# Gates o and z as token-major strips of seven products; branch gates and convolutions as filler in the attention, their results in DRAM

## The chip, the core and the metric

One core of a Trainium2 chip runs the whole program. The engines are TensorE (PE, matmuls and transposes, with its weight loads as PEld), VectorE (DVE), ScalarE (ACT), GpSimd (POOL) and SyncE (SP, which here only issues DMA transfers). The metric is the device time of one execution in microseconds, less is better. Times are the median of several runs; the profile and the trace come from one profiled execution.

## The reference

A decoder block on 512 tokens of 1024 channels, in fp32. Its columns of `w_in` make an mLSTM branch (4 heads of 256), a sparse-attention branch (8 heads of 64) and two merge gates.

```python
hN = _rmsnorm(x, norm_g)
p = _split_in(hN @ w_in)          # m_q m_k m_v m_o m_z: 1024 columns each; g_a g_b: 1024 each; the rest for attention
mq = silu(_causal_dwconv(p["m_q"], conv_q_w, conv_q_b))     # 4 taps along the tokens
mk = silu(_causal_dwconv(p["m_k"], conv_k_w, conv_k_b))
mh = _head_layernorm(_mlstm(mq, mk, p["m_v"], i, f), mh_norm_g)
ya = sigmoid(p["m_o"]) * mh * silu(p["m_z"])
yn = _nsa(...)                                               # compressed, selected and sliding attention, gated
yb = yn * silu(p["n_z"])
merged = sigmoid(p["g_a"]) * (ya @ w_branch_a) + sigmoid(p["g_b"]) * (yb @ w_branch_b)
return _rmsnorm(x + merged @ w_out, final_norm_g)
```

## The kernel before

**Products.** Every fp32 operand is split into a high part (`wh`, `hTh`) and a low part (`wl`, `hTl`), and a product is three matmuls: high by high, high by low, low by high (L214, L216, L218). The normalised input stands in SBUF as `hTh` and `hTl`, [128, 8, 512]: channel within a block, block, token. `weights` (L156) loads 512 KB of raw weights by SyncE's queue into `wr`; ScalarE copies the high part to `wh`, VectorE subtracts for the low part `wl` (L145). Each of the three has three buffers.

**Jobs and filler.** `cols(c0, post)` (L222) makes a job: 128 columns of `w_in` with all tokens, 8 blocks by 3 = 24 matmuls of 512 columns into one PSUM bank, and then `post`, which works on the bank. The result is channel-major, [128 channels, 512 tokens]. Jobs go into `stream` (class `Stream`, L176), which runs the load and the split of a job's weights ahead of its matmuls and gives out the matmuls one step at a time. Attention and mLSTM take such steps between their own matmuls, so that PE has work while the other engines prepare the next of its operands: `tick` (L984) takes 4 steps, or work of the side list; mLSTM takes 6 after a piece of a head (`stream.step(6)`) and 30 before the transposes of a head (`NORM_FILL`). PE, GpSimd and SyncE get their final order from a scheduler; ScalarE and VectorE keep the order of the program (`ordered`, L84).

**The stages** and when they run, by the trace: the start with normalisation and transposes (0 to 30 us); the first projections (30 to 77); attention (77 to 271), 16 units in the loop at L1031, with filler from the stream; two branch-gate jobs (271 to 284); the value strips (284 to 322); four convolution jobs (322 to 343); four mLSTM heads (343 to 499, each some 41.6 us, loop at L1314); branch a with the last gates (499 to 560); the output product (560 to 613) and the tail.

**What fills attention.** `some` (L759) adds eight o jobs and eight z jobs. `gate_o` (L591) puts tanh of its half into `gate` [128, 8, 512]; `gate_z` (L594) multiplies the z path's SiLU, made from a tanh, onto it. Two more jobs there are branch gates: `gate_ab` (L572) keeps sigmoid's tanh for g_a or g_b in SBUF until `branch_a` or `branch_b` uses it. `chores` (L1012) forms sums of quarters of the value columns in DRAM: `begin_sum` copies a quarter by SyncE's queue, `add_to_sum` adds another onto it by an accumulating DMA of GpSimd.

**Strips.** The values (512 x 1024 by 1024 x 1024) are token-major and split 2 by 2 by 2 in each of two token halves' sums: seven products of quarters, with sums of the input (`sum_of_h`, L1132) and of the weights, take the place of eight. `strip_product` (L1190) is one of the seven: two pieces of weights (`wr` of 512 KB each, two blocks by 512 columns), 12 matmuls for each of two row blocks of tokens; 24 in all. The banks are named X, Y and V, and each product's `post` stores a result or copies a partial sum.

**Convolutions.** `conv` (L1251) is a job whose `post` makes four taps along the tokens: one ScalarE pass, three VectorE passes on shifted columns, tanh, one VectorE pass for the SiLU, and the split into high and low. Four of the 16 run ahead of the heads, twelve as filler inside the head before the one that uses them; at a head's end the stream is run until the next head's four are done.

**The rest.** `branch_b` (8 jobs of 12 matmuls) fills the last head. `branch_a` (L1450) multiplies `ya` by `w_branch_a` and merges; six of the g_a gates are computed between its jobs. The output product is again one of seven products; its three weight sums T1, T2, T3 are formed on VectorE while branch a runs (`combine`, L1415; `w21`, L1574), and x for the residual is loaded meanwhile (`fetch_x`, L1485).

Of the kernel before, what the change touches and what calls it, by code (L numbers as in the profile page):

```python
# [28 lines left out]
EARLY = 2  # L29
FIRST = 2  # L30
AHEAD = 6
# [47 lines left out]
def build(  # L79
# [212 lines left out]
    with tc.tile_pool(name="ph0", bufs=2, side="right") as p0, tc.tile_pool(  # L292
# [230 lines left out]
        dve.tensor_scalar(prm[:, :, 10], prm[:, :, 10], 0.25, None, OP.mult)  # L523
# [48 lines left out]
    def gate_ab(base, j, pl):  # L572
        def post(ps):
            s = pl.tile([128, T], F32, name="s", tag="s", bufs=AHEAD if pl is not ybp and pl is not sg0 else 2)
            A(s, ps, AF.Tanh, scale=0.5)
            halves[base, j] = s

        cols(base + j * 128, post)

    gtp = tc.tile_pool(name="gtp", bufs=1, side="right")  # L580
    gate = gtp.__enter__().tile([128, ND, T], F32, name="gate")
# [8 lines left out]

    def gate_o(ct):  # L591
        cols(MO + ct * 128, lambda ps: A(gate[:, ct], ps, AF.Tanh, scale=0.5))

    def gate_z(ct):  # L594
        def post(ps):
            z = rpp.tile([128, T], F32, name="z", tag="z", bufs=1)
            silu2(z, ps, rpp, "slt", 1)
            dve.scalar_tensor_tensor(gate[:, ct], gate[:, ct], 1.0, z, OP.add, OP.mult)

        cols(MZ + ct * 128, post)  # L600
# [156 lines left out]
    gl_ = [(fn, ct) for ct in range(ND) for fn in (gate_o, gate_z)]  # L757

    def some(n):  # L759
        for _ in range(n):  # L760
            if gl_:
                fn, ct = gl_.pop(0)
                fn(ct)

    for base in (GA, GB)[:EARLY]:
        gate_ab(base, 0, ybp)
        if base == GA:
            first_layer(1, 1)
    some(2)
    queries(1)  # L770
    some(3)
    queries(2)
    some(4)
    queries(3)
    some(7)
# [84 lines left out]
    cmp_pool.__exit__(None, None, None)  # L860

# [128 lines left out]
    def new_p():  # L990
# [5 lines left out]
    dram = ctx.enter_context(tc.tile_pool(name="dram", bufs=1, space=bass.MemoryType.DRAM))  # L996
    wsum = [dram.tile([128, 4, 512], F32, name=f"wsum{n}") for n in range(4)]
    wq = [
        [wv[:, 4 * i : 4 * i + 4, MV + 512 * j : MV + 512 * j + 512] for j in range(2)] for i in range(2)
    ]  # L1000

    def begin_sum(n, src):
        tc.keep_in_program_order(nc.sync.dma_start(wsum[n], src))

    def add_to_sum(n, src):
        for q in range(2):
            part = slice(2 * q, 2 * q + 2)
            tc.keep_in_program_order(
                nc.gpsimd.dma_start(wsum[n][:, part], src[:, part], accum_op=OP.add)
            )  # L1010

    chores = deque(  # L1012
        (
            lambda: begin_sum(0, wq[0][0]),
            lambda: begin_sum(2, wq[0][1]),
            lambda: add_to_sum(0, wq[0][1]),
            lambda: begin_sum(1, wq[1][1]),
            lambda: add_to_sum(2, wq[1][1]),
            lambda: begin_sum(3, wq[1][0]),
            lambda: add_to_sum(1, wsum[0]),  # L1020
            lambda: None,
            lambda: add_to_sum(3, wsum[1]),
        )
    )
# [7 lines left out]
    for i, (c, hh, b) in enumerate(units):  # L1032
# [10 lines left out]
        if chores and i > 1:  # L1043
            chores.popleft()()
# [28 lines left out]
    stream.drain()  # L1073
    ap_.__exit__(None, None, None)
# [24 lines left out]
    sg0 = ctx.enter_context(tc.tile_pool(name="sg0", bufs=1))  # L1099
    in_turn = [j for i in range(4) for j in (i, i + 4)]  # L1100
    later = [(GB, 1), (GA, 4)] + [(GB, j) for j in range(2, ND)] + [(GA, j) for j in in_turn[2:]]
    ahead = deque(later[: FIRST + AHEAD])

    def gates_ahead(n, pl):
# [209 lines left out]
    for h in range(4):  # L1314
# [75 lines left out]
        if h < 3:  # L1390
            stream.run()
# [345 lines left out]
```

## Time and profile before

| | us |
|---|---|
| median of 3 runs (lowest, highest) | 623.44 (623.15, 624.19) |
| the profiled execution | 622.71 |
| its span, first to last instruction | 620.8 |
| bytes read from DRAM / written | 68.64 MB / 10.49 MB |
| PE in the start, 0 to 30 us | 27.74 busy |
| PE in the first projections, 30 to 77 us | 47.00 busy of 47.00 |

"Busy" is the time in which at least one instruction of an engine is under way. In a row of a group there stand line, engine, operation, output and inputs, shape, count, then busy us, mean ns of one instruction, and the idle time ahead of them with what ended it. Line 94 is the helper through which ScalarE, VectorE and GpSimd are called, so that groups are told apart by names and shapes. Matmuls overlap in PE: the duration of one is longer than the distance between two.

### The profile page before, as it was taken

Reading aid. Unit: us, or ns where it says so; the run is one execution under the profiler, and the core shown is the slowest. Engines: PE = TensorE matmul, PEld = TensorE weight load, DVE = VectorE, ACT = ScalarE, POOL = GpSimd, SP = SyncE. Lnnn points to the kernel's source line nnn. Section 1 sums busy time; section 2 is a strip of 40 time slices with the busy share of each in tenths; the row PEclk is TensorE's granted clock in tenths of the full one; section 3 lists DMA queues with packets and bytes.
Section 4 is the critical chain, followed back from the end, with each engine's and each line's share of the span. In section 5 each row is a group of like instructions: output and inputs, shape, how many; then the busy total and the mean of one; then the engine's idle time right before and its main releaser. Section 6 shows DMA issues by size and latency. Waiting matters only on the chain.

```text
span 620.8 us, 8484 instructions
## 1 busy us (share of the span) xinstructions
PE 609.2 (98%) x3033; PEld 507.3 (82%) x3033; DVE 449.1 (72%) x860; ACT 326.7 (53%) x621; POOL 85.3 (14%) x167
## 2 busy tenths in 40 slices
PE   8999999999999999999999999999999999999995
PEld 6988888888788888778888888888888888888884
DVE  5876766875876766669677888687787655458885
ACT  5675555556656656646654735545455232234654
POOL 6320012232341231220000000000000100000013
PEclk9999999999999999999999999999999999999999
DMA  9546535338625622123663223223132275333413
GB/s 297 166 112 184 126 104 196 86 91 198 136 57 114 134 71 68 35 68 125 200 185 103 68 69 101 69 69 101 35 101 70 79 247 167 101 106 122 129 34 137
DMA packets 92986, 72.34 MB, mean 117 GB/s; under 512 B 3168, under 2 KB 80132, under 8 KB 92944
## 3 DMA queue, kind: packets, MB, share of 16 engines
q1 hardware_dynamic: 90702, 66.55, 36.8%
q0 software_dynamic: 1664, 4.19, 4.3%
q10 hardware_dynamic: 578, 1.05, 0.5%
q8 instruction: 24, 0.39, 0.3%
q14 instruction: 18, 0.15, 0.1%
HBM read 68.64 MB, written 10.49 MB: 127 GB/s over the span
## 4 chain that ended last, share of the span: by engine, by line
PE 53%; DVE 2%; POOL 1%; ACT 1%; issue 0%; ACTq 0%; DVEq 0%; POOLq 0%
PE pp L218 12%; PE pp L214 12%; PE pp L216 12%; PE ps L174 1%; DVE s L94 1%; PE pp L1206 1%; PE pp L1208 1%; PE pp L1210 1%; PE ps L173 1%; PE ps L172 1%; PE pt L1354 1%; PE pt L1356 1%; PE pt L1355 1%; PE pt L1380 1%; PE pt L1210 1%; PE pt L1208 1%
## 5 line engine op out<-in xcount | busy, mean ns | idle before, releaser
L214 PE MATMUL pp<-hTh,wh 128*128 128x512 f32 (+1 forms) x488 | 191.5, 392 | 0.0
L216 PE MATMUL pp<-hTl,wh 128*128 128x512 f32 (+1 forms) x488 | 190.9, 391 | 0.0
L218 PE MATMUL pp<-hTh,wl 128*128 128x512 f32 (+1 forms) x488 | 190.6, 391 | 0.0
L94 DVE TENSOR_TENSOR wl<-wr,wh 128x1024 fp32r<-128x1024 f32 x92 | 113.2, 1232 | 40.9 <-ACT wh L94 39.5
L94 ACT ACTIVATE wh<-wr 128x1024 fp32r<-128x1024 f32 x92 | 97.2, 1057 | 77.1 <-PE pp L216 48.4
L218 PEld LDWEIGHTS pp<-hTh,wl 128*128 128x128 f32 x488 | 91.9, 188 | 16.5
L214 PEld LDWEIGHTS pp<-hTh,wh 128*128 128x128 f32 x488 | 91.9, 188 | 16.0
L216 PEld LDWEIGHTS pp<-hTl,wh 128*128 128x128 f32 x488 | 92.0, 189 | 15.7
L94 POOL TENSOR_SCALAR P<-P,st,gates 128x128 f32<-128x128 f32 (+1 forms) x64 | 45.3, 721 | 178.7 <-DVE st L94 132.2
L94 ACT ACTIVATE P<-P,st 128x128 f32<-128x128 f32 (+3 forms) x64 | 35.8, 559 | 37.9 <-DVE st L94 37.4
L94 DVE CUSTOM_DVE_ANT_0 P<-ps,cst 128x128 f32<-128x128 f32 (+3 forms) x64 | 30.4, 486 | 22.9 <-PE ps L939 21.8
L94 ACT ACTIVATE pth<-pt 128x512 fp32r<-128x512 f32 (+1 forms) x64 | 26.8, 434 | 28.9 <-PE pt L955 22.2
L94 DVE TENSOR_TENSOR ptl<-pt,pth 128x512 fp32r<-128x512 f32 (+1 forms) x64 | 30.1, 483 | 14.4 <-ACT pth L94 14.3
L94 DVE SCALAR_TENSOR_TENSOR u<-pp,prm,u 128x511 f32<-128x511 f32 (+2 forms) x48 | 35.7, 745 | 0.8
L94 POOL TENSOR_TENSOR rlr<-va,mhalf 128x4 f32<-128x4 f32 x4 | 5.1, 1285 | 208.6 <-DVE va L94 208.6
L94 ACT ACTIVATE th<-u 128x512 f32<-128x512 f32 x16 | 10.1, 631 | 39.5 <-DVE u L94 39.5
L955 PE MATMUL pt<-cst,P 128*128 128x128 f32 x160 | 28.9, 277 | 1.6 <-POOL P L94 1.0
L955 PEld LDWEIGHTS pt<-cst,P 128*128 128x128 f32 x160 | 20.1, 141 | 11.6 <-DVE ptl L94 4.9
L214 PE MATMUL pp<-yah,wh 128*128 128x512 f32 x64 | 24.9, 389 | 0.0
L216 PE MATMUL pp<-yal,wh 128*128 128x512 f32 x64 | 24.9, 389 | 0.0
L218 PE MATMUL pp<-yah,wl 128*128 128x512 f32 x64 | 24.9, 389 | 0.0
L968 PE MATMUL po<-ptl,vsw 128*128 128x512 f32 (+1 forms) x64 | 21.2, 332 | 0.0
(377 smaller groups left out, 1104.9 us busy)
## 6 DMA issues: line engine op xcount, KB each, us to landing
wr<-w_in SPq DMA_DIRECT2D x66, 512.0 KB, 3.9
wsum<-w_in SPq DMA_DIRECT2D x4, 1024.0 KB, 6.0
wr<-wsum SPq DMA_DIRECT2D x8, 512.0 KB, 4.3
wr<-w_out SPq DMA_DIRECT2D x8, 512.0 KB, 3.8
wr<-w_branch_a SPq DMA_DIRECT2D x8, 512.0 KB, 3.8
wsum<-w_in POOLq DMA_DIRECT2D x4, 512.0 KB, 8.2
wsum<-wsum POOLq DMA_DIRECT2D x4, 512.0 KB, 9.1
wr<-w_branch_b SPq DMA_DIRECT2D x4, 512.0 KB, 3.5
```

Source lines behind the costliest of these rows:

```text
L94: ins = fn(*args, **kw)
L172: pe.matmul(ps, a, c, start=start and i == 0, stop=False)
L173: pe.matmul(ps, a, d, start=False, stop=False)
L174: pe.matmul(ps, b, c, start=False, stop=stop and i == n - 1)
L214: pe.matmul(ps, a, c, start=k == 0, stop=False)
L216: pe.matmul(ps, a, d, start=False, stop=False)
L218: pe.matmul(ps, b, c, start=False, stop=k == nk - 1)
L955: pe.transpose(pt[:, (qb - kb) * 128 : (qb - kb) * 128 + 128], P[:, POFF[qb] + kb * 128 : POFF[qb] + kb * 128 + 128], ident,)
L968: pe.matmul(po[:, kb * 128 :], vl, tl[:, :n], start=False, stop=False)
L1206: pe.matmul(ps, a, c, start=begin, stop=False, skip_group_check=not first)
L1208: pe.matmul(ps, a, d, start=False, stop=False, skip_group_check=not first)
L1210: pe.matmul(ps, b, c, start=False, stop=k == 3, skip_group_check=not first)
```

## The change

**The o and z columns become strips.** `gate` is now [128, 4, 1024], token-major. The seven products of a strip are held in a class, once for each of v, o, z; `opening` makes the first two products, `rest` the other five.

```diff
-    for base in (GA, GB)[:EARLY]: ...
-    some(2) ... some(3) ... some(4) ... some(7)
+    class Strip:
...
+        def opening(self, pre=((), (), (), ())):
+            w = self.w
+            strip_product(of_h(0), from_w(w, 0, 0), self.X, True, self.after1, pre[:2])
+            strip_product(of_h(1), from_w(w, 1, 0), self.X, False, self.after2, pre[2:])
...
+            strip_product(of_sum(1), l5, self.V, True, self.after5, pre)
+            strip_product(of_sum(2), l6 if self.first is None else seeded, self.Y, False, self.after6)
+            strip_product(of_sum(3), l3, self.V, False, self.after3)
+            strip_product(of_sum(4), l7, self.Y, False, self.after7, whole=True)
+            strip_product(of_h(3), l4, self.Y, False, self.after4)
...
+    def put_o(tb, half, ps, part=None):
+        if part is not None:
+            dve.tensor_tensor(part, ps, part, OP.add)
+        g = gate[:, tb, half * 512 : half * 512 + 512]
+        A(g, ps if part is None else part, AF.Tanh, scale=0.5 if part is None else -0.5)
+
+    def put_z(tb, half, ps, part=None):
+        g = gate[:, tb, half * 512 : half * 512 + 512]
+        if part is None:
+            s = raws((0, 3)[tb % 2], (T,), "zs")
+            A(s, ps, AF.Silu)
+        else:
+            s = part
+            dve.tensor_tensor(s, ps, s, OP.add)
+            A(s, s, AF.Silu, scale=-1.0)
+        dve.scalar_tensor_tensor(g, g, 1.0, s, OP.add, OP.mult)
...
+    sv.opening(pre=((1,), (), (), ()))
+    so.opening(pre=((), (), (), (2,)))
+    sv.rest(pre=((3,), (4,)))
+    so.rest((o_sum1, lambda q: o_onto(1, 1, q), o_last, lambda q: halves_of(F[q]), lambda q: o_onto(1, 0, q)))
+    sz.opening()
+    sz.rest()
```

The sums of weights for v and z are made in DRAM during attention (16 chores, from unit 0 on, where nine stood from unit 2 on). Those for o are made in SBUF between the products, in a buffer E of 128 x 4 x 512 and two F:

```diff
+    def o_onto(i, j, q):
+        dve.tensor_tensor(piece_of(E, q), piece_of(E, q), raw_of(i, j, q), OP.add)
+        return halves_of(piece_of(E, q))
```

In the o strips' last five products PE's order, with the names' numbers kept (S20 and S21 are high and low part of a sum of the input, `wh` and `wl` a piece of the weights), reads:

```order
L1240 MATMUL pp_3545<-wh_3550,S20_3132 128x512
L1242 MATMUL pp_3545<-wl_3551,S20_3132 128x512
L1244 MATMUL pp_3545<-wh_3550,S21_3133 128x512
L1240 MATMUL pp_3543<-wh_3571,S20_3132 128x512
L1240 MATMUL pp_3545<-wh_3571,S20_3132 128x512
L1240 MATMUL pt_3554<-wh_3592,S30_3134 128x512
L1240 MATMUL pt_3561<-wh_3592,S30_3134 128x512
L1242 MATMUL pp_3543<-wl_3572,S20_3132 128x512
L1244 MATMUL pp_3543<-wh_3571,S21_3133 128x512
```

Four matmuls on two pieces' high parts (wh_3571, wh_3592) stand there ahead of the first on the low part wl_3572. Before, these columns were jobs inside attention.

**What fills attention now** is ten branch gates and eight convolutions, those of heads 0 and 1. Their results go to DRAM by SyncE's queue.

```diff
+    def gate_ab(base, j):
         def post(ps):
+            s = stg.tile([128, T], F32, name="s", tag="s", bufs=2)
             A(s, ps, AF.Tanh, scale=0.5)
+            away[base, j] = dram.tile([128, T], F32, name=f"away{base}_{j}")
+            nc.sync.dma_start(away[base, j], s)
...
+            both = pl.tile([128, 2, T], F32R, name="hl", tag="hl", bufs=2)
+            split(u, both[:, 0], both[:, 1])
+            if e == 0:
+                qk[i, h] = dram.tile([128, 2, 2, T], F32, name=f"qk{i}{h}")
+            nc.sync.dma_start(qk[i, h][:, :, e], f(both))
```

VectorE in attention, before, around a z job (z and gate are the job's; P, st the softmax, ptl the low half of the transposed probabilities, wl the low part of weights):

```order
L94 ISA P,st<-ps,cst 128x512
L94 ISA st 128x1
L94 RECIPROCAL st<-st 128x4
L94 TENSOR_TENSOR ptl<-pt,pth 128x512
L94 TENSOR_TENSOR wl<-wr,wh 128x1024
L94 SCALAR_TENSOR_TENSOR z<-sl,pp 128x512
L94 TENSOR_TENSOR ptl<-pt,pth 128x384
L94 SCALAR_TENSOR_TENSOR gate<-gate,z 128x512
```

And with the change, around a convolution (u, th and hl are its own; the three lengths 511, 510, 509 are the shifted taps):

```order
L92 TENSOR_TENSOR wl<-wr,wh 128x1024
L92 SCALAR_TENSOR_TENSOR u<-pp,prm,u 128x511
L92 TENSOR_TENSOR ptl<-pt,pth 128x128
L92 SCALAR_TENSOR_TENSOR u<-pp,prm,u 128x510
L92 ISA P,st<-ps,cst 128x128
L92 ISA st 128x1
L92 SCALAR_TENSOR_TENSOR u<-pp,prm,u 128x509
L92 ISA P,st<-ps,cst 128x128
L92 ISA st 128x1
L92 ISA P,st<-ps,cst 128x256
L92 ISA st 128x1
L92 SCALAR_TENSOR_TENSOR u<-th,u 128x512
```

Where two operations of a z job stood among the softmax's and the halves' operations, five of a convolution stand (the fifth, `hl<-u,hl`, follows some rows on).

**mLSTM.** The two gate jobs between attention and the strips are gone. After the strips come the four convolutions of head 2; those of head 3, the last six gates, all `branch_b` and the first six blocks of two `branch_a` jobs are the heads' filler (372 steps; the heads take 360), and the extra run at a head's end is gone. Each head reads its q and k back (`fetch_qk`), and two chores of the sums of `w_out` follow it:

```diff
+        if h < 3:
+            fetch_qk(h + 1)
+        for _ in range(2):
+            chores.popleft()()
...
+            nt = num[:, tb, 0:256]
+            A(nt, nt, AF.Identity, bias=nb[:, tb : tb + 1], scale=rho[:, tb : tb + 1])
+            dve.tensor_tensor(nt, nt, gate[:, tb, h * 256 : h * 256 + 256], OP.mult)
+        if h < 3:
+            decay(h + 1)
         stream.step(NORM_FILL)
...
+            gain = prm[:, ct, 10:11]
+            A(ya(ct), pt, AF.Copy, scale=gain)
+            dve.scalar_tensor_tensor(yal[:, ct], pt, gain, f(ya(ct)), OP.mult, OP.subtract)
-        while h < 3 and h + 1 not in done:
-            stream.step(1)
-        if h < 3:
-            stream.run()
```

SyncE's queue before, from the first convolution to branch a, held only weights:

```order
L159 DMA wr<-w_in 128x8x128 x22
L159 DMA wr<-w_branch_b 128x4x256 x4
```

With the change, where head 0's scores are done (qk00 to qk11 are the tiles of q and k, `wsumout` the sums of `w_out`, `away` a gate's place in DRAM):

```order
L1365 DMA qk00_4321<-qk01_2147 128x1024
L1365 DMA qk01_4322<-qk01_2147 128x1024
L1365 DMA qk10_4325<-qk11_2715 128x1024
L1365 DMA qk11_4326<-qk11_2715 128x1024
L1029 DMA wsumout1_4329<-w_out 512x1x512
L609 DMA qk03_4319<-hl_4316 256x1x512
L1029 DMA wsumout3_4331<-w_out 512x1x512
L580 DMA away6944_1_4415<-s_4413 128x512
L157 DMA wr_4569<-w_in 128x8x128
L157 DMA wr_4665<-w_in 128x8x128
```

Four reloads, two copies and two stores now stand ahead of the weights wr_4569.

**Branch a and the output product.** The six gate jobs there are gone; `branch_a` reads g_a's tanh and branch b's result from DRAM, and two of its jobs have only the last two blocks left. T1 to T3 are gone: the output product loads its weight sums from DRAM (`from_sums`), whose signs differ, so that `partway` and `piece` multiply one half by -0.5 and `sums` subtracts in another order. `AHEAD` goes from 6 to 8. In the whole program PE has 2975 matmuls in place of 3023.

More of the change, by code (lines that the diff above doesn't have):

```diff
@@ L756, in build @@
     first_layer(1, 0)
[L757 to L769, printed above, removed]
-    queries(1)
[L771 to L775, printed above, removed]
+    gate_job()
+    first_layer(1, 1)
+    gate_job(3)
+    queries(1)
+    for n in (1, 2, 3):
+        conv_job()
+        gate_job()
+        if n == 1:
+            conv_job()
+            queries(2)
+        elif n == 3:
+            conv_job()
+            queries(3)
+    for _ in range(3):
+        gate_job()
+        conv_job()
     def log_forget():
@@ L994, in new_p, with quarters, begin_sum, add_to_sum @@
         )
[L996 to L1005, printed above, removed]
+    def quarters(w, c0):
+        return [[w[:, 4 * i : 4 * i + 4, c0 + 512 * j : c0 + 512 * j + 512] for j in range(2)] for i in range(2)]
+    wov = w_out[0].rearrange("(k p) c -> p k c", p=128)
+    parts_of = {"v": quarters(wv, MV), "o": quarters(wv, MO), "z": quarters(wv, MZ), "out": quarters(wov, 0)}
+    wsum = {}
+    def begin_sum(w, n, src):
+        wsum[w, n] = dram.tile([128, 4, 512], F32, name=f"wsum{w}{n}")
+        tc.keep_in_program_order(nc.sync.dma_start(wsum[w, n], src))
+    def add_to_sum(w, n, src):
         for q in range(2):
@@ L1097, in build @@
         pool.memset(f(vals(h)[:, :, 257:258]), 0.0)
[L1099 to L1104, printed above, removed]
[L1105 to L1106 removed]
+    gtp = tc.tile_pool(name="gtp", bufs=1, side="right")
+    gate = gtp.__enter__().tile([128, NT, D], F32, name="gate")
     def quarter(t, i):
@@ L1463, in gen @@
                 me[j] = t
-                for i in range(4):
-                    if not left and i in me and i + 4 in me:
-                        sums(i)
-            stream.add(lambda: weights(wav[:, :, j * 128 : j * 128 + 128]), gen)
-        turns = deque(in_turn)
-        left = deque(later[FIRST + AHEAD :])
-        n = 0
-        while turns:
-            if left_to_add := later[FIRST + AHEAD + n : FIRST + AHEAD + n + 1]:
-                gate_into(*left_to_add[0], fp.tile([128, T], F32, name="g", tag="g", bufs=6))
-                if n in (1, 3):
-                    combine(n // 2)
-                n += 1
-                if n < 3:
-                    continue
-            branch_a(turns.popleft())
+                if j > 3:
+                    sums(j - 4)
+            stream.add(load, gen)
+        for j in in_turn:
+            branch_a(j)
         xo, fg = {}, {}
```

402 lines of the change are left out of this document (216 added, 186 removed).

## The prediction

> **What bounds the kernel now.** I read the page's head first, to see which engine has no spare time, and whether its clock is whole.
>
> ```profile
> span 620.8 us, 8484 instructions
> PE 609.2 (98%) x3033; PEld 507.3 (82%) x3033; DVE 449.1 (72%) x860; ACT 326.7 (53%) x621; POOL 85.3 (14%) x167
> PEclk9999999999999999999999999999999999999999
> ```
>
> TensorE is busy for 98% of the span at the full granted clock; VectorE, the next, has a quarter of its time free. The list of PE's waits says how much of the rest is waiting:
>
> ```profile
> PE ps L317 <- DMA grow<-norm_g: 2.3, 1, 2.3
> PE pt L955 <- POOL P L94: 1.0, 2, 0.6
> PE pt L955 <- DVE ptl L94: 0.5, 2, 0.3
> PE po L967 <- ACT pth L94: 0.3, 1, 0.3
> PE ps L691 <- PE pp L216: 0.3, 1, 0.3
> ```
>
> 2.3 us at the start, 2.1 us after it. So time leaves this kernel only with matmuls, and returns only with new waits of PE. The view by stretches of time shows where room is; its columns are each engine's busy us (instructions), the granted clock, the DMA share and GB/s. The stretches are attention, the two gate jobs behind it, the value strips, four convolution jobs, the four mLSTM heads, branch a, the output product, and the tail.
>
> ```profile
> 77.00:271.00 194.00, 191.73 (x1004) 157.50 (x1003) 136.43 (x331) 111.94 (x265) 53.12 (x72) 1.00 0.42 106
> 271.00:284.00 13.00, 13.00 (x60) 10.75 (x59) 10.18 (x11) 5.97 (x8) 0.33 (x8) 1.00 0.26 78
> 284.00:322.00 38.00, 38.00 (x169) 31.32 (x168) 30.63 (x32) 24.60 (x32) 0.00 (x0) 1.00 0.58 174
> 322.00:343.00 21.00, 21.00 (x95) 17.38 (x94) 15.58 (x21) 9.41 (x13) 0.00 (x0) 1.00 0.41 114
> 343.00:499.00 156.00, 156.00 (x783) 131.25 (x782) 121.41 (x237) 77.21 (x140) 5.14 (x4) 1.00 0.28 78
> 499.00:560.00 61.00, 61.00 (x270) 50.49 (x269) 32.88 (x42) 19.45 (x26) 0.00 (x0) 1.00 0.54 159
> 560.00:613.00 53.00, 53.00 (x244) 44.09 (x243) 44.52 (x62) 26.86 (x42) 6.12 (x17) 1.00 0.26 81
> 613.00:620.80 7.80, 0.71 (x6) 0.51 (x5) 3.24 (x11) 3.01 (x6) 2.09 (x6) 0.82 0.64 238
> ```
>
> PE idles 2.27 us in attention, and nowhere else between the start and the tail.
>
> **What PE loses.** The o and z columns were two products of 512x1024 by 1024x1024, 16 jobs of 24 matmuls of 512 columns. As strips of seven products each takes 7 x 24 = 168 matmuls where 192 stood. The order of instructions counts 3023 matmuls before and 2975 after; the 48 that go all have 512 columns, and every other shape keeps its count. A matmul's row says 0.39 us, but they overlap; what counts is the distance of the starts, here in the value strips:
>
> ```profile
> 299.80 0.39 PE L1206 MATMUL pp<-wh,S 128*128 128x512 f32 x1
> 300.03 0.39 PE L1208 MATMUL pp<-wl,S 128*128 128x512 f32 x1
> 300.26 0.39 PE L1210 MATMUL pp<-wh,S 128*128 128x512 f32 x1
> ```
>
> 0.23 us; over the stretch 284 to 322, 38.39 us (with the last one's 0.39) by 169 give 0.227. **48 x 0.227 = 10.9 us less.** That is sure as long as PE stays full, so the rest of the sum asks what it will wait for.
>
> **Attention (bound 0 to 17.9, taken 1.6).** Sixteen o and z jobs leave it, and eight convolutions and eight more branch gates enter it. Per job the other engines pay:
>
> ```profile
> L94 DVE SCALAR_TENSOR_TENSOR u<-pp,prm,u 128x511 f32<-128x511 f32 (+2 forms) x48 | 35.7, 745 | 0.8
> L94 DVE SCALAR_TENSOR_TENSOR u<-th,u 128x512 f32<-128x512 f32 x16 | 11.0, 686 | 7.1 <-ACT th L94 7.1
> L94 DVE TENSOR_TENSOR qkl<-u,qkh 128x512 fp32r<-128x512 f32 x16 | 11.0, 686 | 2.1 <-ACT qkh L94 2.1
> L94 DVE SCALAR_TENSOR_TENSOR z<-sl,pp 128x512 f32<-128x512 f32 x8 | 5.4, 681 | 1.3 <-ACT sl L94 1.3
> L94 DVE SCALAR_TENSOR_TENSOR gate<-gate,z 128x512 f32<-128x512 f32 x8 | 5.5, 682 | 0.1
> L94 ACT ACTIVATE u<-pp,prm 128x512 f32<-128x512 f32 x16 | 12.2, 762 | 0.0
> L94 ACT ACTIVATE th<-u 128x512 f32<-128x512 f32 x16 | 10.1, 631 | 39.5 <-DVE u L94 39.5
> L94 ACT ACTIVATE qkh<-u 128x512 fp32r<-128x512 f32 x16 | 9.9, 621 | 3.1 <-DVE u L94 3.1
> ```
>
> A convolution costs VectorE 3 x 0.745 + 2 x 0.686 = 3.61 us, a z job 0.681 + 0.682 = 1.36. Eight of each: 28.9 - 10.9 = 17.9 us more; VectorE goes from 136.4 of 194 us (70%) to 154.3 (80%). ScalarE adds 8 x (0.762 + 0.631 + 0.621) = 16.1, less 8 tanh of some 0.6, and goes from 58% to about 64%. If no delayed piece is waited for, the cost is nothing; if each is, all 17.9. PE's 2.27 idle us are the nearest row. Queueing behind an in-order engine grows roughly with share over spare: 0.70/0.30 = 2.3 against 0.80/0.20 = 4.0, times 1.7; 2.27 becomes 3.9, 1.6 more. That is an estimate. Gate and convolution results now leave by SyncE's queue, each store waiting there for ScalarE or VectorE with weight loads queued behind it. That hides while three raw weight tiles last: an attention job takes some 9 us (194 us by 22 jobs), a load 3.9.
>
> ```profile
> wr<-w_in SPq DMA_DIRECT2D x66, 512.0 KB, 3.9
> wsum<-w_in SPq DMA_DIRECT2D x4, 1024.0 KB, 6.0
> L94 DVE TENSOR_TENSOR wl<-wr,wh 128x1024 fp32r<-128x1024 f32 x92 | 113.2, 1232 | 40.9 <-ACT wh L94 39.5
> L94 ACT ACTIVATE wh<-wr 128x1024 fp32r<-128x1024 f32 x92 | 97.2, 1057 | 77.1 <-PE pp L216 48.4
> q1 hardware_dynamic: 90702, 66.55, 36.8%
> q0 software_dynamic: 1664, 4.19, 4.3%
> ```
>
> **Seam into the strips (0 to 2.3, taken 0.2).** The two gate jobs that followed attention, 48 x 0.227 = 10.9 us of cover, now lie inside it. The value strips start six matmuls after the last head. One piece late costs its split, 1.06 + 1.23 = 2.3; the first two pieces are split before attention ends, so little is left.
>
> **Strips (0 to 9.6, taken 0.3).** They now run for 3 x 168 x 0.227 = 114 us instead of 38. A piece feeds 12 matmuls, 2.72 us; loads of 512 KB at that pace are the 0.58 share at which no wait arose. What is new is that the o strips form weight sums in SBUF: in their last five products (27.2 us) VectorE has 10 splits, 8 sums of the same size and 4 half-size adds, 18 x 1.23 + 4 x 0.68 = 24.9 us, 91%, against 30.63 of 38 (81%) in the old strips. If each sum came late by its own 1.2 us, that is 8 x 1.2 = 9.6. PE's order already takes four matmuls on high halves ahead of a late low half there. Followed piece by piece with these durations, the tightest low half is ready 0.5 us before its matmul, so I stay near the lower end. Two more table loads for the Silu cost ScalarE 2 x 1.28 us (four now stand at 1283 ns), where it has a third of its time free.
>
> ```profile
> L94 ACT ACT_TABLE_LOAD x4 | 5.1, 1283 | 1.3 <-PEq L1727 1.3
> ```
>
> **mLSTM heads (0 to 4.4, taken 0.3).** The next head's q and k come back from DRAM, 2.1 MB, issued when the scores of the head before are done; behind them SyncE has two quarters of w_out (2.1 MB), two stores (0.8) and then weights. q1 moved 66.55 MB in 36.8% of 620.8 us, 291 GB/s when busy: 5.0 MB take 17.2 us. PE has 74 fill matmuls (16.8 us) and most of a head's own work, some 23 us, until the job that needs the next weights, less 2.3 for their split. That fits with 3.5 us over; an accumulating DMA beside it, 1.05 MB at 4.19 MB / (4.3% of 620.8 us) = 157 GB/s, takes 6.7 us, and then it misses by up to 3.2, more where the store's wait adds about 1.2. The second head alone sees both. The normalisation has the same 36 fill matmuls as before; decays of the next head move ahead of them, and VectorE loses eight convolutions here, which is relief without a gain: PE already has 156.00 of 156.
>
> By the Trainium skill's page "DMA: Bandwidth & Descriptors" (section "Issuing engines are not separate DMA queues"), transfers of all engines interleave on the same 16 DMA engines, which puts the accumulating DMA into this sum and speaks against the change. This row, with one such DMA in it, agrees: 0.82 of the DMA time for 151 GB/s. By the rule this term would be 3.2 in place of 0.3, and the total 617.3.
>
> ```profile
> 138.00:150.00 12.00, 11.98 (x63) 9.79 (x62) 8.58 (x19) 6.49 (x15) 4.47 (x5) 1.00 0.82 151
> ```
>
> **Branch a and output (0 to 2.3, taken 0.2).** Six gate columns leave; matmuls do not change. g and b come from DRAM, 1 MB each 5.4 us, 190 GB/s, about the 159 to 174 borne now. In the output product x (2.1 MB, 7.2 us at 291 GB/s) is loaded ahead of one weight piece; one late split is 2.3. The subtractions that formed the w_out sums on VectorE fall away, cover without a gain.
>
> **Sum.** -10.9 + 1.6 + 0.2 + 0.3 + 0.3 + 0.2 = -8.3. The profiled execution took 622.7 us (span 620.8 and 1.9 around it), so **614.4**. The median of the runs shown is 0.7 higher; I leave that to the range.
>
> **Rivals.**
> - *Clean: every new load finds cover.* For it: PE full in all stages but attention, and VectorE stalled it there for 0.5 us in all. 622.7 - 10.9 = 611.8, or 612.5 from the median.
> - *Transfers jam.* The heads' reloads, the w_out sums and x collide as worked out: 611.8 + 1.6 + 4.4 + 2.3 = 620.1 at the upper bounds, 618 in the middle. Against it: the mLSTM stretch uses 0.28 of the DMA time now. The skill's page "TensorE: Matmul & The Clock Gate" (section "HAM oscillation — how this bites in real kernels") says that a gap of PE over about 3.4 us throttles the clock, worth up to some 1.7 us more by its figures, an estimate. The trace has no such gap before the tail, where the clock's row falls to 0.82.
> - *Slower: VectorE's extra time in attention reaches PE.* Every transposed probability block needs VectorE's low half, and only some four fill matmuls (0.9 us) stand between PE's steps. If all 17.9 us are waited for, 622.7 - 10.9 + 17.9 = 629.7; it turns slower from 10.9/17.9 = 61% of it on. Against it: z jobs put 10.9 us into the same queue, and PE waited 0.5 us for VectorE there.
> - *The change does less than it says.* The order of instructions shows the 48 matmuls gone; what is left is a PE no longer back to back for an unseen reason: 622 to 624.
>
> **How the numbers follow.** Forecast (613 to 617) 0.60; clean 0.18; jam 0.13; slower 0.06; nothing 0.03. The range 611.3 to 620.5 takes in the first three and the upper bounds of transfers; the slower rival stays outside. About 0.2% is what a measurement of this kernel can tell from no change. Faster by more: 0.60 + 0.18 + nearly all of 0.13 = 0.90; slower 0.07 (0.06 and some of the last case); within 0.2%: 0.03.
>
> **What would show it.** PE's records number 48 fewer and starts in the strips stay 0.227 us apart. Attention's stretch keeps PE near 98%, VectorE near 80%; its PE waits on VectorE or ScalarE sum to 2 to 4 us. In the strips' waits, any row of PE on wl is the o sums. In the second mLSTM head, a PE wait on wh or wl whose own wait is a DMA would show the jam. The forecast is wrong if attention grows by more than 5 us, or the strips take more than 116 us.

## The result and the profile after

| | before | changed |
|---|---|---|
| median, us (lowest, highest) | 623.63 (622.95, 626.53), 6 runs | 615.66 (614.96, 617.11), 6 runs |
| the profiled execution, us | 622.71 | 615.59 |
| its span, us | 620.8 | 613.8 |

The ratio is 0.9868 (95% interval 0.9847 to 0.9890): 8.0 us less by the medians, 7.1 by the two profiled executions. Forecast were 8.3 less than the profiled execution of before, 614.4, and 611.3 to 620.5.

The head of the changed kernel's page, as quoted of before:

```profile
span 613.8 us, 8697 instructions
PE 600.3 (98%) x2985; PEld 498.9 (81%) x2985; DVE 459.6 (75%) x870; ACT 357.4 (58%) x667; POOL 101.9 (17%) x183
...
PEclk9999999999999999999999999999999999999998
...
q1 hardware_dynamic: 98542, 112.69, 58.1%
q0 software_dynamic: 4992, 12.58, 13.0%
```

48 records of PE fewer (3033 to 2985), 8.9 us less of busy time, the same 98%: PE still sets the time. The transfers grew from 72 MB to 127 MB in all. PE's list of waits:

```profile
PE ps L315 <- DMA grow<-norm_g: 2.2, 1, 2.2
PE pt L979 <- POOL P L92: 1.0, 2, 0.6
PE pp L1678 <- DVE T4l L92: 0.6, 2, 0.4
PE pt L979 <- DVE ptl L92: 0.4, 1, 0.4
PE po L991 <- ACT pth L92: 0.3, 1, 0.3
PE ps L716 <- PE pp L214: 0.3, 1, 0.3
PE ps L962 <- DVE st L92: 0.2, 1, 0.2
```

One row is new in kind: T4l, the low half of the output product's last weight sum. By stage (attention; the three strips; four convolution jobs; heads with branch a; the output product; the tail), with the columns of before:

```profile
77.70:274.70 197.00, 194.46 (x1011) 158.80 (x1009) 153.01 (x356) 121.97 (x283) 63.09 (x80) 1.00 0.67 172
274.70:389.60 114.90, 114.90 (x505) 94.24 (x504) 89.46 (x92) 72.77 (x92) 0.33 (x8) 1.00 0.65 198
389.60:411.40 21.80, 21.80 (x98) 18.05 (x97) 16.38 (x21) 9.82 (x15) 0.00 (x0) 1.00 0.94 299
411.40:566.00 154.60, 154.60 (x781) 131.42 (x780) 112.91 (x234) 79.66 (x148) 12.15 (x12) 1.00 0.87 256
566.00:605.60 39.60, 38.98 (x181) 31.83 (x180) 30.11 (x40) 21.61 (x34) 5.75 (x16) 1.00 0.53 179
605.60:613.80 8.20, 0.28 (x3) 0.08 (x1) 3.18 (x11) 3.14 (x6) 2.12 (x7) 0.72 0.64 238
```

Heads and branch a now use 0.87 of the DMA time (0.28 in the heads and 0.54 in branch a before), and PE is busy in all of that stretch.

**Where the time went, by stage.** The borders are starts of matmuls, read from each trace: the first of a 24-matmul job, of a score, of a strip, of the decays, of the output product, and the last matmul. "Due" is the stage of before less its matmuls that went, or plus those that came, at 0.227 us (attention -48, strips +336, heads and branch a -336).

| stage, us | before | due | changed | over |
|---|---|---|---|---|
| start and first projections | 77.80 | 77.80 | 78.48 | +0.7 |
| attention up to the strips | 205.69 | 194.79 | 196.22 | +1.4 |
| strips | 38.17 | 114.44 | 114.97 | +0.5 |
| four convolutions | 21.76 | 21.76 | 21.76 | 0.0 |
| heads and branch a | 231.78 | 155.51 | 154.64 | -0.9 |
| output product | 38.24 | 38.24 | 39.53 | +1.3 |
| tail | 7.35 | 7.35 | 8.21 | +0.9 |
| span | 620.8 | 609.9 | 613.8 | +3.9 |

If the 48 matmuls are worth their 10.9 us (z_eight, below, tests their price), 3.9 us come back: the question for the experiments is by what.

### The profile page after: what moved, and what is told of

Same layout as the page of the kernel before. It is cut to its first block, busy times and chain, and to the rows that moved or that the text cites. A ratio compares the mean times of both kernels' runs of the same rounds, so it can differ in the third digit from the quotient of the medians.

```text
span 613.8 us, 8697 instructions
## 1 busy us (share of the span) xinstructions
PE 600.3 (98%) x2985; PEld 498.9 (81%) x2985; DVE 459.6 (75%) x870; ACT 357.4 (58%) x667; POOL 101.9 (17%) x183
## 4 chain that ended last, share of the span: by engine, by line
PE 48%; DMA 3%; DVE 2%; ACT 1%; issue 1%; POOL 1%; SPq 0%; ACTq 0%; POOLq 0%
PE pp L214 6%; PE pp L216 6%; PE pp L212 5%; PE pp L1240 3%; PE pp L1242 3%; PE pp L1244 3%; PE pp L1561 2%; PE pp L1557 2%; PE pp L1559 2%; PE pt L1242 2%; PE pt L1244 2%; PE pt L1240 2%; DMA wr<-w_out 2%; PE ps L1240 1%; PE ps L1242 1%; PE ps L1244 1%
## 5 line engine op out<-in xcount | busy, mean ns | idle before, releaser
L92 DVE TENSOR_TENSOR wl<-wr,wh 128x1024 fp32r<-128x1024 f32 (+2 forms) x104 | 126.4, 1217 | 55.8 <-ACT wh L92 50.6
L92 ACT ACTIVATE wh<-wr 128x1024 fp32r<-128x1024 f32 (+2 forms) x104 | 108.1, 1041 | 59.2 <-PE pp L214 12.0
L212 PE MATMUL pp<-hTh,wh 128*128 128x512 f32 (+1 forms) x360 | 141.5, 393 | 0.0
L214 PE MATMUL pp<-hTl,wh 128*128 128x512 f32 (+1 forms) x360 | 141.1, 392 | 0.0
L216 PE MATMUL pp<-hTh,wl 128*128 128x512 f32 (+1 forms) x360 | 141.0, 392 | 0.0
L216 PEld LDWEIGHTS pp<-hTh,wl 128*128 128x128 f32 x360 | 67.9, 189 | 11.4
L212 PEld LDWEIGHTS pp<-hTh,wh 128*128 128x128 f32 x360 | 67.9, 189 | 10.9
L214 PEld LDWEIGHTS pp<-hTl,wh 128*128 128x128 f32 x360 | 68.0, 189 | 10.7
L92 DVE TENSOR_TENSOR ptl<-pt,pth 128x512 fp32r<-128x512 f32 (+1 forms) x64 | 29.9, 481 | 11.3 <-ACT pth L92 11.1
L991 PE MATMUL po<-pth,vsw 128*128 128x512 f32 (+1 forms) x64 | 20.6, 322 | 0.3 <-ACT pth L92 0.3
L1561 PE MATMUL pp<-yah,wl 128*128 128x512 f32 x50 | 19.5, 389 | 0.0
```

The source lines that it names most:

```text
L92: ins = fn(*args, **kw)
L212: pe.matmul(ps, a, c, start=k == 0, stop=False)
L214: pe.matmul(ps, a, d, start=False, stop=False)
L216: pe.matmul(ps, b, c, start=False, stop=k == nk - 1)
L991: pe.matmul(po[:, kb * 128 :], vl, th[:, :n], start=b == 0 and kb == 0, stop=False)
L1561: pe.matmul(ps, q, ya(k), start=False, stop=k == ND - 1)
```

## The experiments

The same table for every kernel run (one profile each; times in us, ratios to the kernel before with 95% intervals). "Head 2" runs from the decays of one head to those of the next; "late" is heads with branch a. Each run's ratio is to the kernel before as it ran beside it, on the same chip.

| run | attention | strips | head 2 | late | product | tail | median | ratio |
|---|---|---|---|---|---|---|---|---|
| changed, first profile | 196.22 | 114.97 | 29.15 | 154.64 | 39.53 | 8.21 | 615.66 | 0.9868 (0.9847 to 0.9890) |
| again | 196.42 | 115.88 | 30.71 | 156.19 | 39.27 | 8.22 | 615.93 | 0.9884 (0.9872 to 0.9897) |
| x_on_pool | 196.42 | 114.80 | 30.36 | 155.84 | 38.91 | 8.23 | 616.07 | 0.9882 (0.9870 to 0.9895) |
| x_spread | 196.47 | 114.98 | 29.14 | 156.14 | 39.47 | 8.24 | 617.68 | 0.9911 (0.9895 to 0.9927) |
| convs_later | 195.18 | 115.23 | 30.01 | 161.53 | 40.21 | 8.23 | 620.28 | 0.9942 (0.9929 to 0.9955) |
| t4_own | 196.42 | 115.08 | 30.08 | 155.56 | 46.17 | 7.96 | 618.60 | 0.9917 (0.9904 to 0.9929) |
| sums_early | 196.39 | 119.98 | 29.13 | 154.63 | 39.50 | 8.21 | 621.04 | 0.9957 (0.9942 to 0.9973) |
| z_eight | 196.34 | 120.63 | 29.13 | 154.63 | 40.50 | 8.15 | 622.69 | 0.9985 (0.9971 to 0.9999) |
| heavy | 194.48 | 115.46 | 29.14 | 154.63 | 39.49 | 8.21 | 615.63 | 0.9870 (0.9848 to 0.9893) |
| light | 196.62 | 114.88 | 29.15 | 154.65 | 39.57 | 8.23 | 616.20 | 0.9886 (0.9874 to 0.9899) |
| x_t4_pool | 196.26 | 115.79 | 29.47 | 163.98 | 38.11 | 7.60 | 622.75 | 0.9985 (0.9974 to 0.9996) |
| shift | 196.21 | 115.92 | 29.15 | 155.17 | 42.51 | 8.24 | 617.03 | 0.9905 (0.9884 to 0.9927) |
| t4_sp_x_pool | 196.25 | 115.09 | 29.13 | 154.61 | 39.43 | 7.96 | 615.60 | 0.9879 (0.9862 to 0.9895) |

### What a run alone moves: again

The changed kernel, unaltered.

> The changed kernel once more, beside the three variants below, and a second profile of it. Its start (first instruction to the first matmul of a job of 24) took 27.33 us in the first profile against 26.66 before. If that 0.67 us is the run's and not the kernel's, it moves here by as much again; if it is the kernel's, it stays within 0.1. The attention stage should again take 196.2 us, the output product 39.5 and the tail 8.2, each within 0.3, if these are properties of the order and not of the run.

The start took 26.71 us, as before: the 0.7 us of the first profile is the run's. Attention, product and tail repeat within 0.3. Two waits are new, in the strips and in the second head:

```profile
PE ps L170 <- DVE Dm L92: 1.3, 1, 1.3
...
PE pp L1678 <- DVE T4l L92: 0.7, 1, 0.7
PE pp L1242 <- DVE wl L92: 0.7, 1, 0.7
```

The row on wl stands in the last of the value strip's products. VectorE, which keeps the program's order, waited 1.12 us there for a raw piece of an o sum, and the low half that PE needed stood behind it:

```profile
317.73 1.23 DVE L92 TENSOR_TENSOR E<-E,wr 128x1024 f32<-128x1024 f32 x1 [1.12 <-DMA wr<-w_in]
318.88 1.22 DVE L92 TENSOR_TENSOR wl<-wr,wh 128x1024 fp32r<-128x1024 f32 x1
```

x_t4_pool and shift have the same row (0.6 and 0.7 us). So one kernel's strips and second head differ from run to run, here by 0.9 and 1.6 us; a stage's difference of that size between two profiles says nothing.

### The price of a matmul: z_eight

```diff
-    sz.opening()
-    sz.rest()
+    for t0 in (0, 2):
+        for j in range(2):
+            bk = (sz.X, sz.Y, sz.V, lambda l: sz.at(("W", l), PP))[t0 + j]
+            put = lambda l, t0=t0, j=j, bk=bk: put_z(t0 + l, j, bk(l))
+            strip_product(of_h(t0), from_w("z", 0, j), bk, True, none)
+            strip_product(of_h(t0 + 1), from_w("z", 1, j), bk, False, put)
```

> z alone as eight products of quarters, with no sums of the input or weights (its weight sums are still formed in DRAM, unused): 192 matmuls where 168 stand. Theory that the gain is the matmuls' count at 0.227 us each: the strips go from 115.0 to 120.4 us, all other stages stay, and the time rises by 5.4 us to about 621. Rival: the strips' time is set by their transfers or splits (two pieces of 16 in place of 14 for z); then it rises by less, or by the 2 x 2.3 us of two splits.

The strips grew by 5.66 us (120.63 against 114.97) where 24 x 0.227 = 5.45 were due: the main term stands. The time rose by 6.8 against the run again. In the profile 1.0 us more stands in the output product (40.50), which no edit of this kernel touches and which took 39.3 to 40.2 in other runs that agree there; the rest of the 6.8 isn't placed.

### Attention: VectorE's load or something else

```diff
     # convs_later: in attention, four of the eight
-        conv_job()
+        gate_job()
...
     # in the heads
-    for _ in range(4):
-        conv_job()
-        gate_job()
-    gate_job(2)
+    conv_job(8)
+    gate_job(2)
```

> Four of attention's eight convolutions change places with four branch gates of the mLSTM heads. Theory that attention's loss of 1.4 us is VectorE's: its busy time there falls by 4 x 3.61 = 14.4 us (153 to 139, before: 146 in a stage longer by two jobs), attention falls from 196.2 to about 195.0 and the time by 1.2 us; the heads, where PE never waits, stay as they are. Rival, that the loss comes from transfers (16 weight-sum steps where nine stood, and the stores): attention stays at 196.2 and the time as it is.

Attention came out at 195.18, as the theory had it. The time rose, for a reason that no theory had named: the last piece of the fourth head's q and k was stored at 487.17 us, their reload was issued at 492.18 and landed at 503.60. PE's waits in the heads:

```profile
PE ps L172 <- DMA qk<-qk: 1.8, 1, 1.8
PE ps L170 <- DVE Dm L92: 1.0, 1, 1.0
PE ps L170 <- DMA qk<-qk: 0.8, 1, 0.8
```

With the clock at 0.79 from 501 to 507 us and 0.92 to 513, they make up most of the 6.9 us by which heads and branch a grew. Then the load was doubled instead.

```diff
     # heavy: after the three passes of a convolution in attention
+            if h < 2:
+                u2 = pl.tile([128, T], F32, name="u2", tag="u2", bufs=1)
+                for s in (1, 2, 3):
+                    dve.scalar_tensor_tensor(u2[:, s:], ps[:, : T - s], w(3 - s), u[:, s:], OP.mult, OP.add)
```

> Each of attention's eight convolutions makes its three passes on shifted columns twice, the second time into a tile that nobody reads: 24 passes more of some 0.74 us, 17.7 us more of VectorE in attention (153 of 197 to 171, 87%). Theory of queueing behind an in-order engine with spare time (loss as share over spare): 0.78/0.22 = 3.5 becomes 0.87/0.13 = 6.7, the waits of about 3.9 us double, attention grows by some 3.5 us. Rival, that PE pays VectorE's time in full once it is over 80%: it grows by up to 17.7 us. Rival, that VectorE does not count: under 0.5 us.

All three theories missed: attention took 194.48, 1.7 us *less*. Taking passes away was the counter-test.

```diff
     # light: two of three passes left out
-            for s in (1, 2, 3):
+            for s in (1, 2, 3) if h > 1 else (1,):
```

> Attention's eight convolutions make only the first of their three passes on shifted columns (two taps of q and k of heads 0 and 1 are left out): 16 passes of some 0.74 us, 11.9 us of VectorE, less in attention (153 to 141). Doubling the passes made attention 1.9 us shorter, not 3.5 longer, and took PE's order in attention another way. Theory now: attention's waits of some 4 us go by where the transposes stand in PE's order against VectorE's and GpSimd's queue, not by VectorE's sum; then attention comes out anywhere between 194 and 198 us, no shorter for the lighter load than the 195.2 of fewer convolutions. The first theory (share over spare, 0.71/0.29 = 2.5 against 3.5): 1.1 us shorter, about 195.2, and the shorter stalls before transposes go first.

196.62, no shorter. The same stretch (77.7 to 274 us) of the changed kernel, of light and of heavy, in this order; VectorE is the third pair:

```profile
77.70:274.00 196.30, 193.76 (x1007) 158.23 (x1006) 152.45 (x355) 121.83 (x282) 63.09 (x80) 1.00 0.67 172
```
```profile
77.70:274.00 196.30, 193.12 (x1005) 157.99 (x1005) 142.25 (x339) 122.08 (x282) 61.86 (x80) 1.00 0.66 171
```
```profile
77.70:274.00 196.30, 194.81 (x1016) 160.50 (x1016) 166.45 (x379) 122.76 (x284) 62.35 (x80) 1.00 0.67 173
```

VectorE at 142, 152 and 166 us goes with attention at 196.6, 196.2 and 194.5 (in heavy the last 1.6 us of the stretch are strips already), and convs_later, with 140, stood at 195.2. **VectorE's sum does not set the loss.**

Still it is VectorE that PE waits for, and most of the wait hides from PE's own rows: it stands before the weight loads (PEld) of the transposes, which need the low half of the probabilities (ptl), and of the scores (st). Before, changed, heavy, in attention:

```profile
PEld pt L955 <- DVE ptl L94: 4.9, 12, 0.7
PEld ps L938 <- DVE st L94: 0.4, 1, 0.4
```
```profile
PEld pt L979 <- DVE ptl L92: 5.9, 13, 0.9
PEld ps L962 <- DVE st L92: 1.3, 4, 0.4
```
```profile
PEld pt L983 <- DVE ptl L92: 3.0, 8, 0.5
PEld ps L966 <- DVE st L92: 2.4, 5, 0.7
```

The two rows sum to 5.3, 7.2 and 5.4 us, and attention is 1.4 over its due in the changed kernel and 1.7 shorter again in heavy. PE's order in attention differs from the changed kernel's in convs_later, light and heavy, most in heavy, since the scheduler places the matmuls anew around other work, and the places of these waits differ with it. That the order is the cause is likely, but no run held the load and changed the order alone. The transfers do not set it: in sums_early, below, PE's order in attention is the changed kernel's, the second half of attention used 0.96 of the DMA time in place of 0.66, and attention took 196.39.

### The output product and the tail

In the changed kernel, VectorE, ScalarE, SyncE and PE around T4:

```profile
591.20 0.34 SPq L1732 DMA_DIRECT2D wr<-wsumout  x1
...
595.77 1.22 DVE L92 TENSOR_TENSOR T4l<-wr,T4h 128x1024 fp32r<-128x1024 f32 x1
595.92 1.06 ACT L92 ACTIVATE T4h<-wr 128x1024 fp32r<-128x1024 f32 x1 [0.79 <-DMA wr<-wsumout]
...
597.04 0.50 PE L1678 MATMUL pp<-T4l,mx 128*128 128x512 f32 x1 [0.27 <-DVE T4l L92]
...
598.23 1.22 DVE L92 TENSOR_TENSOR T4l<-wr,T4h 128x1024 fp32r<-128x1024 f32 x1
...
599.50 0.50 PE L1678 MATMUL pp<-T4l,mx 128*128 128x512 f32 x1 [0.35 <-DVE T4l L92]
```

The last piece is issued at 591.20, ScalarE waits for it, and PE waits for the half that VectorE makes behind it. First theory: x, eight loads ahead on SyncE's queue.

```diff
     # x_on_pool
-                    nc.sync.dma_start(t, x[0, tb * 128 : tb * 128 + 128, hs])
+                    nc.gpsimd.dma_start(t, x[0, tb * 128 : tb * 128 + 128, hs])
     # x_spread: x in its own tiles, one with each job of branch a
+                next_x()
+                return wa, g, b
```

> The eight loads of x go out on GpSimd's queue in place of SyncE's; nothing else moves. Theory: in the output product, the x loads stand on SyncE's queue ahead of the last eight weight pieces, those come late, the last weight sum's low half (T4l) is late by 0.9 us and the chain to the end starts from it, which costs the output product 1.3 and the tail 0.8 us. Then product and tail come back to the 38.2 and 7.4 us of before, and the time falls by about 2 us. Rival: the pieces are late because seven products now take all their weights through three raw tiles, where three sums stood in SBUF before; then x's queue is without effect, product and tail stay at 39.5 and 8.2, and the time stays within 0.3 us.

> The eight loads of x get tiles of their own and go out one with each job of branch a, on SyncE's queue (the tiles of the sums fall from eight to two, those of g from six to five, to make room). Theory: as above, product 38.2 and tail 7.4, time down by 2 us, if branch a bears 2.1 MB more in its 35 us (it moves 250 GB/s now, and would move 310). Rival of three raw tiles: no change. A third way: the transfers of branch a become late and PE waits there; then the product gains 2 us and branch a loses some.

Neither run bears the theory out: the product came to 38.91 and 39.47, the tail stayed at 8.23 and 8.24, and x_spread took 1.5 us more in branch a (45.97). x's place is worth 0.4 to 0.6 us of the product at most. In both traces ScalarE's splits of weights stood in step with PE from 575 us on, none but those of T4 itself waiting for a transfer, and still the last T4 piece went out at 591.25 and 591.53. It waits for a raw tile, one of three, as the rival had it.

```diff
     # t4_own
-            raw = wp.tile([128, 2, 512], F32, name="wr", tag="wr", bufs=3)
+            raw = f(p4[1][:, ks])
             nc.sync.dma_start(raw, wsum["out", 4][:, ks])
```

> The raw last weight sum of the output product (two pieces) is loaded straight into the tile of its low half and split there in place, so that it waits for no raw tile; all else, x's place too, stays. The two runs on x showed T4l late with x off the queue and with x early. Theory now: the second T4 piece is issued at 591.2 us only because its raw tile, one of three, comes free with an earlier split; the landing (4.7 us) and the two halves (1.06 and 1.22 us) behind that make PE wait and set the chain to the end. Then the output product falls from 39.3 to 38.3 and the tail from 8.2 to 7.4, the time by 1.5 to 2 us. Rival: ScalarE and VectorE are too full in the last 15 us to split two pieces there at all (before, one raw piece and T2 were split); then the product stays above 39 and the tail at 8.2.

The T4l wait was gone and the product 6.6 us longer: with T4's load early on its queue, SyncE sent x at 574 in place of 569, on top of the next weights, which then took 8 us to land. PE's row, behind which 6.8 us went by at half the clock (last section):

```profile
PE ps L1677 <- ACT wh L92: 2.5, 1, 2.5
```

So both at once.

```diff
     # x_t4_pool: both of the above, and
-            nc.sync.dma_start(raw, wsum["out", 4][:, ks])
+            nc.gpsimd.dma_start(raw, wsum["out", 4][:, ks])
```

> Both of the output product's edits together, on GpSimd's queue: x's eight loads, and the last weight sum's two pieces straight into the tile of its low half. Theory: each alone failed for the other's reason. With x off SyncE's queue alone every piece was split as soon as PE freed a tile, and the second T4 piece still waited for a raw tile (issued at 591.3, landed 595.9); with T4's own tile alone SyncE's queue carried T4 early and x 5 us later, on top of the third product's weights. Together no load of the last 25 us stands behind x or a raw tile of T4: product 38.3 us, tail 7.4 to 8.0, time down by 1.5 us against the changed kernel. Rival: with T4's split early in branch a, ScalarE or VectorE makes branch a late, which stood at 44.46 in nearly all runs; then that stage grows by as much.

Product 38.11 and tail 7.60, the values of before (38.24, 7.35) but for 0.2 in the tail. But the rival was right too: branch a took 53.47 in place of 44.46, and loads of the product that wait for nothing in branch a can get ahead in those 9.0 us. So the run does not show that the two edits alone made the product short.

```profile
POOL T4l L1732 <- DMA wr<-w_branch_a: 9.5, 1, 9.5
...
ACT T4h L92 <- DMA g<-away: 10.4, 1, 10.4
...
PE pp L1557 <- ACT wh L92: 6.4, 1, 6.4
```

T4's split had been placed early on ScalarE, which keeps the program's order; T4, issued at 530.98, landed at 540.00, and every later split of weights stood behind it. The last try put T4's load back on SyncE's queue.

> x's loads on GpSimd's queue and the last weight sum loaded straight into the tile of its low half, but that load on SyncE's queue, where the run with T4's own tile alone had it: branch a took its usual 44.46 us there, against 53.47 with T4's load on GpSimd's queue, where ScalarE stood 10.4 us in front of the late T4. Theory: with both obstacles gone and T4 landed before ScalarE turns to it, the product takes the 38.1 us and the tail the 7.6 that the run with both on GpSimd's queue showed, and branch a stays at 44.46: the time falls by 1.5 to 2 us, to about 614, less if strips or the second head have one of their late weights (up to 1.5 us each, by the run). Rival: T4's megabyte on SyncE's queue makes the second and third products' weights late by itself, whatever x does; then the product stays over 40 us, as with T4 alone (46.2).

Branch a was back at 44.46 and the T4l wait gone, but the product took 39.43, its small waits now on the low halves of other pieces: without the 9 us of delay the theory of two obstacles failed for the product, and its rival (over 40 us) did too. For the tail a part holds: it took 7.60 to 7.96 in the three runs in which T4 has a tile of its own, and 8.15 to 8.24 in all others. 615.60 us is the changed kernel's time: no version here beats it.

### The heads' transfers

```diff
     # sums_early: w_out's sums in attention's second half
+        for _ in range(2 if i > 7 else 1):
+            chores.popleft()()
     # shift: in the heads, dealt otherwise
-        for _ in range(2):
+        for _ in range((0, 2, 3, 3)[h]):
             chores.popleft()()
```

> The eight steps that form w_out's sums in DRAM move from the mLSTM heads into the second half of attention (two steps for each of units 8 to 15). Theory: in the second head a weight load issued at 432 us needs 12.9 us (first profile) or 14.6 (second) to land, and where it needs more than 13 ScalarE, in order, stands at its split and the decay behind it is late, so that PE waits up to 1.5 us for Dm. Without those sums the load lands within 10 us, the second head takes 29.1 us in every profile, and the time falls by 0 to 1.5 us with less spread between runs. Attention, if its loss is VectorE's alone, stays at 196.3 us though it moves 12 MB more. Rival: attention's transfers count too; then it grows by over 0.5 us and takes the gain back.

> The eight steps of w_out's sums in the mLSTM heads are dealt 0, 2, 3, 3 to the four heads in place of 2, 2, 2, 2. Theory: the second head's wait for Dm (0 to 1.5 us, four of six profiles) comes from the weight load that lands 13 to 15 us after its issue, beside head 0's sums; without them there it lands within 10 us, and the second head takes 29.1 us as it did where the sums lay in attention. Time down by 0 to 1.5 us, if the sums are still ready for the output product. Rival: the jam moves to the third head, whose weights then stand beside the sums (30 us or more there), or the last sum is late and the output product pays.

What they go against is seen in the changed kernel's queues between 411 and 500 us:

```profile
q0 software_dynamic: 1366, 3.13, 23.3%
...
wr<-w_in SPq DMA_DIRECT2D x6, 512.0 KB, 12.3
```

and, before, in the heads (343 to 499 us):

```profile
wr<-w_in SPq DMA_DIRECT2D x17, 512.0 KB, 3.9
```

A weight load that took 3.9 us before takes 12.3 there (medians). In the run again the load issued at 432.4 landed at 447.05, and ScalarE stood before its split with the next head's decay behind it:

```profile
444.27 0.63 ACT L92 ACTIVATE Sh<-Dm 128x512 fp32r<-128x512 f32 x1
447.13 1.06 ACT L92 ACTIVATE wh<-wr 128x1024 fp32r<-128x1024 f32 x1 [2.23 <-DMA wr<-w_in]
448.10 0.58 ACT L92 ACTIVATE s<-pp 128x512 f32<-128x512 f32 x1
449.95 0.83 ACT L92 ACTIVATE Sh<-Dm 128x384 fp32r<-128x384 f32 x2 [1.27 <-DVE Dm L92]
```

The ten profiles that keep the heads as the change has them show this link by its size. Where that load landed within 12.9 us (six profiles), the second head took 29.1 us; where it took 13.35, 13.97, 14.25 and 14.62, ScalarE waited 0.98, 1.59, 1.86 and 2.23 us for it, and the head took 29.47, 30.08, 30.36 and 30.71. From about 0.65 us on, PE pays ScalarE's wait in full. Without the sums beside it, in shift, the load issued at 438.98 landed after 3.96 us; the one issued at 439.03 in the changed kernel took 11.68. Both kernels took 29.1 us in the second head, but so did six of the ten (the expectation's "four of six" should have been three of seven), so one profile each does not show that they remove the wait, and how often it comes is not measured. Both gave more back elsewhere. In sums_early the sums of attention's end ran into the strips, where ScalarE stood 3.06 us before the split of a late piece, an o gate behind it came late, and PE, which needed the gate's bank, waited 3.0 us (starts 3.4 apart); then its clock fell.

```profile
290.00:295.00 5.00, 1.96 (x8) 1.32 (x8) 2.11 (x3) 2.44 (x4) 0.00 (x0) 0.97 0.76 268
295.00:300.00 5.00, 5.00 (x17) 3.88 (x17) 4.51 (x5) 1.60 (x2) 0.00 (x0) 0.68 0.40 134
```

5 us at 0.68 are 1.6 us lost: 3.2 and 1.6 of the strips' 5.0 us more. In shift the output product took 42.51. The last sum was ready at 517 us, 40 us ahead of the first load of a sum, so the rival's late sum is not the reason; three weight loads issued behind x, from 574.89 us on, took about 8 us to land, as in t4_own. Whether the other dealing made them late or the run did is open.

## Why the prediction was right, point by point

- **48 matmuls, 10.9 us: right.** PE's records are 48 fewer, and z_eight prices 24 of them at 5.66 us, so that 48 are worth 10.9 to 11.3.
- **Attention, 1.6: the size was right (1.4), the reason was not.** The step failed that took it from "share over spare" of VectorE: with more work on VectorE attention became shorter, with less it did not, so the size was luck. The waits that grew are for VectorE, 1.9 us more before PE's weight loads, but they go with where those stand and not with VectorE's sum. The sign named for it did not come: PE's own waits for VectorE and ScalarE sum to 0.9 us (0.8 before), not 2 to 4. The rival *VectorE's extra time reaches PE*, up to 17.9 us, falls with it, as does its turning point at 61%.
- **Seam and strips, 0.5: right in size**, 0.5 in the first profile, 1.4 in the second. The sign named for it, a PE row on wl in the strips, is the 0.7 us of the run again. It came from the o sums, but not by VectorE's 91%: by a raw piece that landed late, with VectorE waiting for it.
- **mLSTM, 0.3: the mechanism was right, in the head named.** It reached PE by another way than was worked out: not by a wait on the late half of a fill job, but by the decay behind that split on ScalarE. The term was 0 in the first profile, 1.6 in the second and in between in three others. That heads and branch a came out 0.9 *below* their due in the first was not foreseen and is not explained.
- **Branch a and output, 0.2: mis-sized.** It measured 1.3 in the product and 0.9 in the tail, just inside the bound of 2.3. "x is loaded ahead of one weight piece" saw a part of it, the 0.4 to 0.6 of x_on_pool. The subtractions on VectorE that fell away were called "cover without a gain"; but with them T2, the sum of the last product, had left SBUF, and now waits for a raw tile. In the changed kernel's trace the two waits on T4l and the slow starts behind them make up 1.2 of the product's 1.3 us; what would bring it back without a new wait no run here shows. The tail, given no term, is 0.3 to 0.6 shorter with T4 in a tile of its own; the rest of its 0.9 is open.
- **The jam** as a whole did not come (2.2 of its 6.7 us at the bounds in the first profile), though the DMA share rose from 0.28 in the heads and 0.54 in branch a to 0.87 over both. What the Trainium skill's page "DMA: Bandwidth & Descriptors" says of transfers that interleave on the same engines (section "Issuing engines are not separate DMA queues") agrees with the 12.3 us against 3.9. The 3.2 us that the prediction worked out by that rule were not paid in the heads, 0 to 1.6 were.

That the total came so near is in part luck: a term of 2.2 that was taken as 0.2 met a heads' term below zero in the profile, and the forecast started from a profiled execution that was 0.9 us faster than the median of before, so 8.3 stood against 7.1 by profile and 8.0 by the medians. The run's own spread (614.96 to 617.11) is as wide as these terms.

## What to carry to other kernels

Count the bottleneck engine's instructions and price them by the distance of their starts: that part of this forecast held. Then list every value that moves from SBUF to DRAM, and ask which ring of buffers its reload must now wait for, and which in-order engine stands at its split: this is where the gain came back, and why each repair of one queue moved the wait to the next. A busy share, VectorE's here, is not a price, and moving it in either direction is a cheap way to find out. And where a fault shows in some profiles only, as in the second head, set the size of its cause against the size of the loss over all profiles: that tells more than one run with the cause taken away.

## What the runs showed of the hardware

Ahead of the tail, PE's clock fell to half around a gap in four of the runs, and stayed there for one of two lengths. In sums_early (matmul starts 3.4 us apart from 290.7 us on) and in convs_later (1.2 and 2.2 apart within 4 us) it was half for 3.4 us; in t4_own (2.9 apart from 584.8 on) and x_t4_pool (6.8 apart from 535.5 on) for 6.8. Sums_early, t4_own, x_t4_pool, and x_t4_pool right behind:

```profile
294.74:298.15 3.41, 3.41 (x10) 2.63 (x9) 3.41 (x4) 0.80 (x1) 0.00 (x0) 0.50 0.45 154
```
```profile
587.19:594.01 6.82, 5.80 (x13) 4.24 (x14) 4.69 (x5) 2.62 (x3) 0.00 (x0) 0.50 0.50 147
```
```profile
539.75:546.58 6.83, 4.07 (x9) 2.77 (x10) 5.27 (x7) 4.43 (x6) 0.00 (x0) 0.50 0.92 289
546.58:551.00 4.42, 4.42 (x21) 3.63 (x20) 4.32 (x10) 2.25 (x3) 0.00 (x0) 1.00 0.75 235
```

In these stretches the 512-column matmuls that did not wait started 0.43 us apart in place of 0.227. The clock need not fall at the end of a gap: in t4_own it fell at 587.19, 0.6 us before the gap's end, in x_t4_pool at 539.75, 2.5 before. Nor does the length of a gap alone set the time at half the clock: 3.4 us in sums_early brought 3.4, 2.9 in t4_own (with 1.3 right behind) brought 6.8. In shift, starts 1.6 and 1.3 us apart within 3 us left the clock at 1.00.

The Trainium skill's page "TensorE: Matmul & The Clock Gate" (section "HAM oscillation — how this bites in real kernels") puts the limit at gaps of some 3.4 us and the throttled time behind one, in its kernel, at some 1.67 us at half the clock. The runs differ from both: PE was idle for 2.5 us in t4_own and 3.0 in sums_early, and the throttled time was 3.4 and 6.8.

A wait of PE of some 3 us thus cost half as much again, or more, in lost clock: 1.6 us in sums_early. Not expected either: the DMA engines at a share of 0.87 for 155 us, with single loads three times as long, and PE without a wait there in the first profile.
